# The remainder of each weight tile by an accumulating transfer on Pool instead of a VectorE subtraction

## The chip, the cores and the metric

The kernel runs on one core of one Trainium2 chip. The metric is the device time of one execution in microseconds; the time before is the median of three runs. An engine's name stands for its in-order instruction queue: TensorE (PE, with its weight loads PEld), VectorE (DVE), ScalarE (ACT), GpSimd (POOL) and SyncE (SP). SyncE only issues transfers; the transfers themselves run on 16 DMA engines.

## The reference

A decoder trunk of two layers over 512 tokens and 1024 channels, in float32. Layer one mixes tokens with a Mamba-2 state-space block (SSD, 8 groups, chunks of 128 tokens), layer two with latent attention (MLA, 8 heads). Each mixing is followed by a layer norm and by a gated feed-forward part (FFN) of hidden width 2816 with a causal depthwise convolution, and that by another layer norm:

```python
for i in range(DEPTH):
    mix = ssd_mixer(h, ...) if i < N_A_LAYERS else mla_attention(h, ..., *shared_kv, cos, sin)
    h = layer_norm(DN_ALPHA * h + mix, ln_mix_g[i], ln_mix_b[i])
    h = layer_norm(DN_ALPHA * h + conv_ffn(h, ...), ln_ffn_g[i], ln_ffn_b[i])
    if i == N_A_LAYERS - 1:
        shared_kv = mla_shared_kv(h, ...)
```

## The kernel before, in words

All matrix products run on TensorE with operands of type float32r. To keep float32's precision, each operand is held as two tiles: a cast to float32r (hi) and the remainder (lo = value - hi). A product is then three passes: hi x hi, lo x hi and hi x lo. In `mm_a` the weight is the stationary operand and the order is: all k tiles with the weight's hi, all with its lo, all with its hi against the activations' lo. In `mm_b` the activations are stationary, and the three passes come for each k tile in turn.

The weights come from HBM as a stream of 228 tiles of up to 128 x 1024 (512 KB), in the fixed order in which they are used. `WStream` handles one tile in three steps:

- `_load` (L47): SyncE issues the transfer of tile i into a staging buffer (`wst`, 3 buffers).
- `_split` (L60, L61): ScalarE casts the stage into `wh`, then VectorE writes `wl` = stage - `wh`. `wh` and `wl` have 6 buffers each (`nb`).
- `get` / `retire`: TensorE uses `wh` and `wl`; `retire` frees their buffers.

After each split, the loads of the next three tiles are issued, so a load waits until all that reads its staging buffer's former tile is done. `ahead` runs splits up to `la` = 4 tiles ahead of the tile in use, as far as the 6 buffers allow. SyncE's queue keeps the order in which the program is written; the queues of the other engines are ordered by a scheduler that plans with costs. SyncE's queue also carries other loads: x at the start, `W` (the decay rows of a group, L501), the layer norms' parameters and the output.

The stream runs through the blocks in this order: in SSD z of group 0 and dt (four small tiles, consumed while x arrives), then for each group four tiles of the convolved projections, two of z and up to two of the output projection; six tiles of the output projection at the end (`OUT_LAST`). Then the first FFN: twice 22 up tiles and 12 down tiles. Then MLA: six tiles of the joint down projection (`dw`), two for the rope part of q (`rw`), two for the values (`vw`), eight of 640 columns for the heads (`hw`), eight of the output projection. Then the second FFN.

In the last part of each FFN (`piece`) the six down tiles stay until the last 128 tokens are done; they are retired one by one there. Each block's first products are with tokens that are already normalised (`k.pend` holds the transposes of the last token tile): the FFN does its first four tiles by halves of the tokens.

The layer norm takes sums on VectorE, squares on ScalarE, and the reciprocal root on Pool (`ln_apply`, L155 and L156); SSD has such a step for each group (L587, L588). Pool has no other part in the main work.

Of the kernel before, what the change touches and what calls it, by code (L numbers as in the profile page):

```python
# [14 lines left out]
ALU = mybir.AluOpType  # L15
# [15 lines left out]
class WStream:  # L31
# [19 lines left out]
    def _split(self, nst=None):  # L51
        nc = self.k.nc
        i = self.split
        while self.loaded <= i:
            self._load()
        f = self.items[i][1]
        s = self.st.pop(i)
        h = self.k.wh.tile([P, 1024], F32R, name="wh")
        l = self.k.wl.tile([P, 1024], F32R, name="wl")
        nc.scalar.copy(h[:, :f], s[:, :f])  # L60
        nc.vector.tensor_tensor(l[:, :f], s[:, :f], h[:, :f], op=ALU.subtract)  # L61
        self.w[i] = (h, l)
        self.split += 1
        while self.loaded < min(len(self.items), self.split + (self.nst if nst is None else nst)):
            self._load()
# [17 lines left out]
class K:  # L83
# [28 lines left out]
        return self.ps.tile([P, 512], F32, name="ps")  # L112

    def mm_a(self, out, w, xts, ts, c0=None, m=P, first=True, last=True):
        """out[m, ts] = W^T x over the k tiles; w = (hi, lo) of [P, nk, m]."""
        nc = self.nc
        wh, wl = w
        nk = len(xts)
        for p, (w, x) in enumerate(((wh, 0), (wl, 0), (wh, 1))):
            for k in range(nk):  # L120
                nc.tensor.matmul(out, w[:, k, :], xts[k][:, x, ts], start=first and p == 0 and k == 0,  # L121
                                 stop=last and p == 2 and k == nk - 1, skip_group_check=True)

    def mm_b(self, out, xt, tsl, wh, wl, start, stop):
        """out[tok, n] += x W for one k tile."""
        nc = self.nc
        nc.tensor.matmul(out, xt[:, 0, tsl], wh, start=start, stop=False, skip_group_check=True)  # L127
        nc.tensor.matmul(out, xt[:, 0, tsl], wl, start=False, stop=False, skip_group_check=True)  # L128
        nc.tensor.matmul(out, xt[:, 1, tsl], wh, start=False, stop=stop, skip_group_check=True)  # L129
# [5 lines left out]
        self.gb = t  # L135

    def add_mix(self, i, hf, ps, scale, last=False):
        """h half <- scale * h half + ps; the last time with its sum over channels."""
        hs = self.h[:, i, hf * 512:(hf + 1) * 512]
        kw = {}  # L140
        if last:
            if i not in self.st:
                self.st[i] = self.lns.tile([P, 6], F32, name="lnst", bufs=4)
            kw["accum_out"] = self.st[i][:, hf:hf + 1]
        self.nc.vector.scalar_tensor_tensor(hs, hs, scale, ps, op0=ALU.mult, op1=ALU.add, **kw)  # L145
# [16 lines left out]
            nc.vector.scalar_tensor_tensor(hv[:, sl], hv[:, sl], rstd, self.gb[:, 1, sl], op0=ALU.mult, op1=ALU.add)  # L162

    def ln_last(self, i, bs, out):
        """The last tile: its second half comes in two pieces (bs); the squares are taken
        about the mean c of the first three quarters, so that only the last quarter's are
        left at the end: var = mean((h - c)^2) - (mu - c)^2."""
        nc = self.nc
        hv = self.h[:, i, :]
        s = self.st.pop(i)  # L170
# [21 lines left out]
            nc.sync.dma_start(out[:, sl], hv[:, sl])  # L192

    def transpose_h(self, i):
        """h[:, i, :] -> ht[k][:, 0/1, i*128:(i+1)*128]."""
        nc = self.nc
        ts = slice(i * P, (i + 1) * P)
        for q in range(2):
            b = self.bank()
            for j in range(4):  # L200
                k = q * 4 + j
                nc.tensor.transpose(b[:, j * P:(j + 1) * P], self.h[:, i, k * P:(k + 1) * P], self.ident)  # L202
            bv = b.rearrange("p (k t) -> p k t", k=4)
            hi = self.htt[:, q * 4:(q + 1) * 4, 0, ts]
            nc.scalar.copy(hi, bv)
            nc.vector.tensor_tensor(self.htt[:, q * 4:(q + 1) * 4, 1, ts], bv, hi, op=ALU.subtract)
# [5 lines left out]


def ffn_items(up, down):
    """up: [44, P, 1024] tiles; down: [2816, 1024]."""
    it = []
    dv = down.rearrange("(k p) n -> p k n", p=P)
    for r in range(2):
        for c in range(r * 11, r * 11 + 11):
            it.append((up[c], 1024))  # L220
            it.append((up[c + HT], 1024))
        for hf in range(2):
            for j in range(0, 11, 2):
                n = min(2, 11 - j)
                k0 = r * 11 + j
                it.append((dv[:, k0:k0 + n, hf * 512:(hf + 1) * 512], n * 512))
    return it
# [17 lines left out]


def ffn(k, ws, base, cwp, gb, la=2, out=None):
    """h <- LN(alpha h + conv_ffn(h)); expects ht of h complete up to k.pend."""
    nc, tc = k.nc, k.tc
    with ExitStack() as c:  # L250
        pool = lambda n, b: c.enter_context(tc.tile_pool(name=n, bufs=b))
# [6 lines left out]
        for r in range(2):  # L258
# [5 lines left out]

            c0 = r * 11
            if k.pend:
                # the first pairs by halves of the tokens: the last tiles are still to come
                bs = [k.bank() for _ in range(4)]
                wv = lambda i: [x.rearrange("p (k m) -> p k m", k=KT) for x in ws.get(n + i)]
                for i in range(4):  # L270
# [78 lines left out]
ZDT = ((0, 1), (1, 4), (4, 7), (7, 8))  # L349
OUT_AT = {2: (0, 1), 3: (2, 3), 4: (4, 5), 5: (6, 7), 7: (8, 9)}  # L350
WARM = 8
# bulk matmul time (us) to let pass before the chain steps s1..s5 and the cumulative dt step
LAG = [18, 13, 6, 5, 11, 13]
OUT_LAST = (10, 11, 12, 13, 14, 15)
DRAM = bass.MemoryType.DRAM


def ssd_items(xbc, zdt, zw, ow):
    """xbc: [32, P, 1024] tiles (16 x, 8 B, 8 C); zdt: [P, 8, 288] (z of group 0, dt); zw: [1024, 2048]; ow: [2048, 1024]."""
    it = []  # L360
    zv = zw.rearrange("(k p) n -> p k n", p=P)
    for a, b in ZDT:
# [13 lines left out]
def ssd(k, ws, base, xT, x, cwp, hv, ngp, gb):  # L376
    nc, tc = k.nc, k.tc
    with ExitStack() as cx:
# [5 lines left out]
        ytp = pool("yt", 7)  # L384
        drp = pool("drp", 1, space=DRAM)

        # parameters
        cw = one.tile([P, 32, 5], F32, name="cw4")
        ng = one.tile([P, 16], F32, name="ng")
        hb = one.tile([P, 3, NH], F32, name="hb")  # L390
# [5 lines left out]
        nc.gpsimd.memset(ones, 1.0)  # L396

        xv = xT.rearrange("(k p) n -> p k n", p=P)
        # the tensor engine's clock rises while the first loads are under way
        warm = k.bank()  # L400
        for _ in range(WARM):
            nc.tensor.matmul(warm[:, :P], k.ident, k.ident, start=True, stop=True)
# [83 lines left out]
            D.update(cum=cum, ecum=ecum, ecl=ecl, wend=wend, cumd=cumd)  # L486

        def bc(t, g, c0, c1, part=P):
            """per-head columns of group g for chunks c0..c1, broadcast over the head's channels."""
            return t[:, c0:c1, g * HPG:(g + 1) * HPG].unsqueeze(3).broadcast_to([P, c1 - c0, HPG, HD])  # L490

        def v4(t, c):
# [117 lines left out]
            todo.append((key, fn, t0, after))  # L610

        def tick(dt_us):
            """account for bulk matmuls; run the chain steps whose inputs had time to come."""
            T[0] += dt_us
            again = True
            while again:
# [29 lines left out]
                tick(2.6)  # L646

        def z_dt():
            """z of group 0 and dt, along with the arrival of x."""
            zs = G[0]["z"] = one.tile([P, NT, GC], F32, name="zs")  # L650
            bs = [k.bank() for _ in range(NT)]
            c = -1
# [49 lines left out]
        for g in range(NG):  # L702
# [31 lines left out]
                k.load_ln(gb)  # L734
            if g in OUT_AT:
                out_block(OUT_AT[g], g == min(OUT_AT))
        # the last rows of out_proj: those at hand before the last chain ends
        early, late = OUT_LAST[:4], OUT_LAST[4:]
        w = [ws.get(n[0] + j) for j in range(len(OUT_LAST))]
        pre = {}  # L740
# [35 lines left out]


def mla_items(dw, vw, rw, hw, ow):
    """dw [6,P,1024]; vw [256,1024]; rw [384,512]; hw [8,P,640]; ow [1024,1024]."""
    it = [(dw[j], 1024) for j in range(4)] + [(dw[j][:, :768], 768) for j in (4, 5)]  # L780
    rv = rw.rearrange("(k p) n -> p k n", p=P)
    it += [(rv[:, 0:2, :], 1024), (rv[:, 2:3, :], 512)]
# [5 lines left out]


def rope_tables(k, pos, freq):  # L790
    """cos, sin of positions x frequencies, [P, NT, 32] with tokens on partitions."""
    nc = k.nc
    c = k.const
    N = NT * 32
# [26 lines left out]


def rope(k, dst, ps, i, nh, tmp):
    """dst[P, nh, 64] = rope of ps[P, nh, 64] (token layout) for token tile i."""
    nc = k.nc
    cos = k.cs[:, 0, i, :].unsqueeze(1).broadcast_to([P, nh, 32])
    sin = k.cs[:, 1, i, :].unsqueeze(1).broadcast_to([P, nh, 32])
# [336 lines left out]
```

## Time and profile before

| | before |
|---|---|
| median of three runs, us | 1373.17 (1373.12 to 1376.29) |
| span of the profiled execution, us | 1373.7 |
| instructions | 17806 |
| VectorE busy, us | 858.3 (62%) |
| ScalarE busy, us | 627.5 (46%) |
| Pool busy, us | 45.4 (3%), 76 instructions |
| moved by transfers | 135.19 MB |
| mean granted TensorE clock | 0.999 |

One execution was profiled. Its busy times count an engine's instructions, not the issuing of transfers. A matmul's end in these rows is modelled, so TensorE's busy time also holds part of its short waits; a gap between the starts of its instructions is the safer sign. In a timeline row stand the start, the duration, the engine, the line, the operation with its output and inputs, the number of such instructions merged, and in brackets the idle time before it with what ended that. In a row of waits stand who waited, for whom, the sum in us, how often, and the longest. Line numbers are those of the kernel before.

### The profile page before, as it was taken

How to read it: one execution, taken by the hardware profiler on the slowest of the kernel's cores; microseconds unless marked ns; L12 is line 12 of the kernel's file. 1: busy time of each engine (PE TensorE's matmuls, PEld its weight loads, DVE VectorE, ACT ScalarE, POOL GpSimd, SP SyncE). 2: the span in 40 equal slices, each digit the busy share in tenths (PEclk: the TensorE clock that was granted, in tenths of full speed). 3: DMA queues.
4: the chain of work that ended last, by engine and by line, in shares of the span. 5: the costliest groups of instructions: out<-in, count | busy, mean ns of one | idle time of the engine just before them, and what ended most of it. 6: DMA issues, size and time to landing. Idle time of an engine off the chain costs nothing.

```text
span 1373.7 us, 17806 instructions
## 1 busy us (share of the span) xinstructions
PE 1359.9 (99%) x7001; PEld 1158.3 (84%) x7001; DVE 858.3 (62%) x1333; ACT 627.5 (46%) x1167; POOL 45.4 (3%) x76
## 2 busy tenths in 40 slices
PE   8999999999999999999999999999999999999997
PEld 8898898898898988888888889778898888888886
DVE  6867676677676766435655366987576552456534
ACT  5668647547554544313443134665254442244421
POOL 0000000000001000000000021000000000000002
PEclk9999999999999999999999999999999999999999
DMA  7532322323321522223232222311052323332211
GB/s 237 186 127 74 108 93 93 108 81 119 108 97 37 177 92 92 100 89 104 93 106 85 85 87 64 91 47 62 31 169 95 105 87 100 97 102 93 97 56 62
DMA packets 49652, 135.19 MB, mean 98 GB/s; under 512 B 4736, under 2 KB 12800, under 8 KB 48032
## 3 DMA queue, kind: packets, MB, share of 16 engines
q1 hardware_dynamic: 49568, 134.05, 29.5%
q8 instruction: 55, 0.90, 0.3%
q14 instruction: 29, 0.24, 0.0%
HBM read 131.87 MB, written 2.16 MB: 98 GB/s over the span
## 4 chain that ended last, share of the span: by engine, by line
PE 96%; DVE 2%; DMA 1%; POOL 0%; ACT 0%; issue 0%; SPq 0%; POOLq 0%; DVEq 0%; ACTq 0%
PE ps L121 49%; PE ps L128 12%; PE ps L127 12%; PE ps L129 12%; PE ps L982 2%; PE ps L562 2%; PE ps L1017 1%; PE ps L664 1%; PE ps L202 1%; PE ps L550 1%; PE ps L573 1%; PE ps L1004 1%; PE ps L508 1%; PE ps L529 1%; DMA W<-cumd 0%; PE ps L596 0%
## 5 line engine op out<-in xcount | busy, mean ns | idle before, releaser
L121 PE MATMUL ps<-ht,wh 128*128 128x512 f32 (+1 forms) x2048 | 464.2, 377 | 0.0
L121 PEld LDWEIGHTS ps<-ht,wh 128*128 128x128 f32 x2048 | 367.7, 188 | 69.4
L61 DVE TENSOR_TENSOR wl<-wst,wh 128x1024 fp32r<-128x1024 f32 (+2 forms) x228 | 266.5, 1174 | 166.0 <-ACT wh L60 165.4
L60 ACT CAST wh<-wst 128x1024 fp32r<-128x1024 f32 (+2 forms) x228 | 229.9, 1013 | 239.3 <-PE ps L129 185.0
L121 PE MATMUL ps<-ht,wl 128*128 128x512 f32 (+1 forms) x1024 | 239.3, 376 | 0.0
L121 PEld LDWEIGHTS ps<-ht,wl 128*128 128x128 f32 x1024 | 184.7, 188 | 35.0
L128 PE MATMUL ps<-wl,gt 128*128 128x512 f32 (+1 forms) x363 | 140.4, 387 | 0.0
L127 PE MATMUL ps<-wh,gt 128*128 128x512 f32 (+1 forms) x363 | 140.0, 386 | 0.0
L129 PE MATMUL ps<-wh,gt 128*128 128x512 f32 (+1 forms) x363 | 138.6, 382 | 0.0
L237 DVE SCALAR_TENSOR_TENSOR acc<-ps,cw,acc 128x511 f32<-128x511 f32 x88 | 65.5, 746 | 99.5 <-ACT acc L236 99.5
L145 DVE SCALAR_TENSOR_TENSOR h<-h,ps 128x512 f32<-128x512 f32 x95 | 63.1, 683 | 73.7 <-PE ps L129 73.6
L429 DVE SCALAR_TENSOR_TENSOR cv<-ps,cw,cv 128x511 f32<-128x511 f32 (+2 forms) x96 | 71.1, 744 | 38.8 <-ACT cv L427 37.9
L236 ACT ACTIVATE acc<-ps,cw 128x512 f32<-128x512 f32 x88 | 68.3, 777 | 39.8 <-PE ps L121 39.8
L127 PE MATMUL ps<-wh,ht 128*128 128x256 f32 (+2 forms) x288 | 85.6, 297 | 0.0
L129 PE MATMUL ps<-wh,ht 128*128 128x256 f32 (+2 forms) x288 | 84.1, 292 | 0.0
L128 PE MATMUL ps<-wl,ht 128*128 128x256 f32 (+2 forms) x288 | 84.1, 292 | 0.0
L127 PEld LDWEIGHTS ps<-wh,gt 128*128 128x128 f32 x363 | 68.1, 188 | 14.8
L129 PEld LDWEIGHTS ps<-wh,gt 128*128 128x128 f32 x363 | 68.2, 188 | 14.3
L128 PEld LDWEIGHTS ps<-wl,gt 128*128 128x128 f32 x363 | 68.3, 188 | 12.8
L243 ACT CAST gt<-acc 128x512 fp32r<-128x512 f32 x44 | 27.3, 621 | 98.8 <-DVE acc L242 98.8
L241 ACT ACTIVATE acc<-acc 128x512 f32<-128x512 f32 x44 | 27.8, 632 | 87.0 <-DVE acc L238 87.0
L238 DVE SCALAR_TENSOR_TENSOR acc<-ps,cw,acc 128x510 f32<-128x510 f32 x88 | 65.6, 748 | 2.8
(222 smaller groups left out, 1709.7 us busy)
## 6 DMA issues: line engine op xcount, KB each, us to landing
wst<-in_up_dram SPq DMA_DIRECT2D x88, 512.0 KB, 3.5
wst<-in_down_dram SPq DMA_DIRECT2D x40, 512.0 KB, 3.6
wst<-in_xbc_dram SPq DMA_DIRECT2D x32, 512.0 KB, 3.8
W<-cumd SPq DMA_DIRECT2D x8, 1024.0 KB, 4.7
wst<-in_sow_dram SPq DMA_DIRECT2D x16, 512.0 KB, 3.3
wst<-in_zw_dram SPq DMA_DIRECT2D x14, 512.0 KB, 3.4
lngb<-in_gb_dram SPq DMA_DIRECT2D x4, 1024.0 KB, 5.8
wst<-in_aow_dram SPq DMA_DIRECT2D x8, 512.0 KB, 3.4
```

Of the source, the lines that this page charges most:

```text
L60: nc.scalar.copy(h[:, :f], s[:, :f])
L61: nc.vector.tensor_tensor(l[:, :f], s[:, :f], h[:, :f], op=ALU.subtract)
L121: nc.tensor.matmul(out, w[:, k, :], xts[k][:, x, ts], start=first and p == 0 and k == 0, stop=last and p == 2 and k == nk - 1, skip_group_ ...
L127: nc.tensor.matmul(out, xt[:, 0, tsl], wh, start=start, stop=False, skip_group_check=True)
L128: nc.tensor.matmul(out, xt[:, 0, tsl], wl, start=False, stop=False, skip_group_check=True)
L129: nc.tensor.matmul(out, xt[:, 1, tsl], wh, start=False, stop=stop, skip_group_check=True)
L145: self.nc.vector.scalar_tensor_tensor(hs, hs, scale, ps, op0=ALU.mult, op1=ALU.add, **kw)
L236: nc.scalar.activation(a, b, AF.Identity, bias=cw[:, ch, 3:4], scale=cw[:, ch, 2:3])
L237: nc.vector.scalar_tensor_tensor(a[:, 1:], b[:, :SEQ - 1], cw[:, ch, 1:2], a[:, 1:], op0=ALU.mult, op1=ALU.add)
L238: nc.vector.scalar_tensor_tensor(a[:, 2:], b[:, :SEQ - 2], cw[:, ch, 0:1], a[:, 2:], op0=ALU.mult, op1=ALU.add)
L241: nc.scalar.activation(ag, ag, AF.Silu)
L429: nc.vector.scalar_tensor_tensor(t[:, d:], b[:, :SEQ - d], cw[:, ch, 3 - d:4 - d], t[:, d:], op0=ALU.mult, op1=ALU.add)
```

## The change

`_split` keeps the cast. The subtraction on VectorE is replaced by two steps: ScalarE writes minus the cast of the stage into `wl` (the same rounding to float32r, of -s), and a transfer issued from Pool's queue adds the stage onto `wl` in place. The staging buffer is now read by ScalarE twice and by that transfer. The rest of the diff takes comments out and is left out here.

```diff
         nc.scalar.copy(h[:, :f], s[:, :f])
-        nc.vector.tensor_tensor(l[:, :f], s[:, :f], h[:, :f], op=ALU.subtract)
+        nc.scalar.activation(l[:, :f], s[:, :f], AF.Copy, scale=-1.0)
+        nc.gpsimd.dma_start(l[:, :f], s[:, :f], accum_op=ALU.add)
         self.w[i] = (h, l)
```

## The prediction

> **What bounds the kernel now.** I read the page first: busy shares, the chain that ended last, the groups, the transfers. The columns of the transfer rows are count, KB each and median us from issue to landing.
>
> ```profile
> PE 1359.9 (99%) x7001; PEld 1158.3 (84%) x7001; DVE 858.3 (62%) x1333; ACT 627.5 (46%) x1167; POOL 45.4 (3%) x76
> ...
> PE 96%; DVE 2%; DMA 1%; POOL 0%; ACT 0%; issue 0%; SPq 0%; POOLq 0%; DVEq 0%; ACTq 0%
> ...
> L61 DVE TENSOR_TENSOR wl<-wst,wh 128x1024 fp32r<-128x1024 f32 (+2 forms) x228 | 266.5, 1174 | 166.0 <-ACT wh L60 165.4
> L60 ACT CAST wh<-wst 128x1024 fp32r<-128x1024 f32 (+2 forms) x228 | 229.9, 1013 | 239.3 <-PE ps L129 185.0
> ...
> q1 hardware_dynamic: 49568, 134.05, 29.5%
> ...
> wst<-in_up_dram SPq DMA_DIRECT2D x88, 512.0 KB, 3.5
> W<-cumd SPq DMA_DIRECT2D x8, 1024.0 KB, 4.7
> wst<-in_sow_dram SPq DMA_DIRECT2D x16, 512.0 KB, 3.3
> lngb<-in_gb_dram SPq DMA_DIRECT2D x4, 1024.0 KB, 5.8
> h<-in_x_dram SPq DMA_DIRECT2D x1, 2048.0 KB, 10.6
> wst<-in_vw_dram SPq DMA_DIRECT2D x2, 512.0 KB, 4.3
> wst<-in_dw_dram SPq DMA_DIRECT2D x2, 384.0 KB, 4.2
> ```
>
> TensorE is busy for 1359.9 of 1373.7 us and is 96% of the chain, so only 13.8 us could be won at all. VectorE, which the change relieves, is busy 62% of the span and 2% of the chain. What matters is therefore whether a remainder tile (wl) still reaches TensorE in time, and whether a staging buffer (wst) comes back in time for the next load. Next I read a steady stretch of the first FFN in the timeline, the time of all engines in a stretch of the second FFN, and what SyncE's queue waits for.
>
> ```profile
> 487.21 1.98 PE L121 MATMUL ps<-ht,wl 128*128 128x512 f32 x8
> 492.65 1.98 PE L121 MATMUL ps<-ht,wl 128*128 128x512 f32 x8
> 496.47 1.05 ACT L60 CAST wh<-wst 128x1024 fp32r<-128x1024 f32 x1 [0.69 <-PE ps L121]
> 1080.00:1320.00 240.00, 240.00 (x1057) 198.20 (x1056) 122.46 (x148) 86.85 (x108) 0.00 (x0) 1.00 0.29 96
> SPq L47 <- DVE wl L61: 1048.6, 209, 32.6
> SPq L501 <- PE ps L562: 50.6, 7, 9.2
> ```
>
> From one wl pass to the next is 492.65 - 487.21 = 5.44 us: TensorE takes a weight tile each 5.44 us. The cast at 496.47 waited for TensorE to leave the buffers of the tile six before it (nb=6), so its wl is wanted five tiles later, over 27 us on. SyncE's loads wait 1048.6 us in sum for the VectorE subtraction: with three staging buffers, the pass that reads the stage last sets when each load may start. In steady state a load has three tiles, 16.3 us, for everything.
>
> **The change, part by part.** *VectorE* loses 228 subtractions, 266.5 us. TensorE visibly waits for VectorE at one place, in SSD:
>
> ```profile
> 107.36 0.70 PE L573 MATMUL ps<-st,cv 128*128 128x256 f32 x2 [2.10 <-DVE yT L600]
> PEld ps L573 <- DVE yT L600: 2.5, 1, 2.5
> ```
>
> That is 2.10 us by the matmul's row and 2.5 by that of the weight load; I take the latter as the greatest gain.
>
> *ScalarE* gains 228 passes of -s, the same size as its casts: 229.9 us, from 627.5 to 857 (62%). *Pool* gains 228 transfer issues. *The 16 DMA engines* gain 228 transfers that read the stage, read wl and write wl.
>
> **T, the time from a finished -s pass to a landed remainder, is the unknown.** No row has an accumulating transfer or one issued by Pool. From below: a plain load of the same 512 KB takes 3.3 us. From above: the 2048 KB load of h takes 10.6 us, more bytes than the three streams of 512 KB. Nearest are the 1024 KB rows, 4.7 and 5.8 us, since an accumulation reads 1024 KB; I take the slower and round up for Pool's issue: T = 6.0 us. The Trainium skill, DMA: Bandwidth & Descriptors, section Anatomy of one DMA — SWDGE (gpsimd) path, gives 2.0 us plus bytes at 436 GB/s for a transfer issued by Pool; counting both reads that is an estimate of 4.4 us, by which the bursts below would cost 20.8 us instead of 35.8.
>
> *Steady state* costs nothing: load 3.5 + cast and -s 2.1 + T fit into 16.3 us up to T = 10.7, and wl has 27 us. The cost lies where tiles are needed in a burst. There a load first waits for the accumulation of the tile three before it, then its own accumulation follows: T counts twice.
>
> *Start.* The third tile (864 columns) is cast, and TensorE reaches its wl:
>
> ```profile
> 10.08 0.92 ACT L60 CAST wh<-wst 128x864 fp32r<-128x864 f32 x1
> 11.43 0.69 PE L664 MATMUL ps<-wl,ht 128*128 128x288 f32 x4
> ```
>
> With the second tile's -s (0.92) ahead of it, its own cast, its -s (0.92 each) and T, wl lands at 12.84 + T: a stall of T + 1.4 = 7.4 us. SyncE's queue also holds the last load of x behind the fourth weight load, which waits for the first accumulation; those columns of x come into use last, behind this stall.
>
> *MLA, down projection.* All six wl buffers are held until the FFN's last tokens, then six tiles are wanted in quick succession, with three staged. The first two casts, the fifth (768 columns, as the sixth), and TensorE at the sixth's wl:
>
> ```profile
> 803.61 2.19 ACT L60 CAST wh<-wst 128x1024 fp32r<-128x1024 f32 x2
> 813.66 0.82 ACT L60 CAST wh<-wst 128x768 fp32r<-128x768 f32 x1
> 817.29 0.34 PE L128 MATMUL ps<-wl,ht 128*128 128x384 f32 x1
> ```
>
> Three casts and three -s of 1.05 from 803.61 end at 809.91; then T, the load of the sixth tile 4.2, its two passes 1.64, and T: 815.75 + 2T against 817.29. Stall 2T - 1.5 = 10.5 us.
>
> *MLA, values.* The second value tile's load waits for the staging buffer of the first rope tile. The rope tile's cast, that load, and TensorE at the wl of the load's tile:
>
> ```profile
> 837.34 1.05 ACT L60 CAST wh<-wst 128x1024 fp32r<-128x1024 f32 x1 [0.83 <-PE ps L129]
> 840.55 0.38 SPq L47 DMA_DIRECT2D wst<-in_vw_dram  x1
> 849.84 0.39 PE L128 MATMUL ps<-wl,cT 128*128 128x512 f32 x1
> ```
>
> 837.34 + 2.1, T, load 4.3, two passes 2.1, T: 845.84 + 2T. Stall 2T - 4.0 = 8.0 us.
>
> *First tiles of each FFN.* Three tiles are staged, the fourth waits for the first one's buffer.
>
> ```profile
> 440.11 2.96 ACT L60 CAST wh<-wst 128x1024 fp32r<-128x1024 f32 x3 [3.11 <-PE ps L129]
> 455.61 1.12 PE L121 MATMUL ps<-ht,wl 128*128 128x256 f32 x8
> 999.01 2.95 ACT L60 CAST wh<-wst 128x1024 fp32r<-128x1024 f32 x3 [3.11 <-PE ps L129]
> 1013.63 1.12 PE L121 MATMUL ps<-ht,wl 128*128 128x256 f32 x8
> ```
>
> 440.11 + 2.1 + T + 3.5 + 2.1 + T = 447.81 + 2T against 455.61: 2T - 7.8 = 4.2 us. Likewise 1006.71 + 2T against 1013.63: 2T - 6.9 = 5.1 us.
>
> *Last down-projection tile of each FFN.* Here the tile has been loaded long before, and T counts once.
>
> ```profile
> 777.56 0.62 ACT L60 CAST wh<-wst 128x512 fp32r<-128x512 f32 x1 [1.74 <-PE ps L129]
> 792.43 1.03 PE L202 MATMUL ps<-ident,h 128*128 128x128 f32 x8
> ```
>
> The second piece of 33 matmuls ends at 792.43; at 5.44/24 = 0.227 us a matmul the first begins at 777.47 and reaches its last wl at 784.5. That lands at 777.56 + 1.24 + T: T - 5.7 = 0.3 us, twice 0.6.
>
> *SSD.* All engines over 250 us of it, and the same matmuls of two groups in the chain:
>
> ```profile
> 150.00:400.00 250.00, 250.00 (x1473) 221.60 (x1473) 178.90 (x244) 151.52 (x362) 6.44 (x10) 1.00 0.30 99
> ```
>
> ```profile
> 208.67 1.30 PE ps L573 x6
> ...
> 262.34 1.30 PE ps L573 x6
> ```
>
> ScalarE is busy 151.5 of 250 us, and a group, 262.34 - 208.67 = 53.7 us, has up to eight tiles, so 8.4 us more of ScalarE work: it stays below 80%. If one -s stands ahead of each group's chain it costs 1.05 x 8 = 8.4 us; if the shorter VectorE work ends the stall shown above it gains 2.5 us. Every tile's buffers come from far ahead, so I take + 1. The W load stands in SyncE's queue behind weight loads that now wait longer; it waits 50.6/7 = 7.2 us for TensorE today, more than the delay of T + 1.05 - 1.2 = 5.9 us, so it is covered; without that cover each of the eight groups could lose what T exceeds 7.3 us by.
>
> *Pool's queue.* The cast, and with it the -s, can wait long for TensorE:
>
> ```profile
> ACT wh L60 <- PE ps L129: 185.0, 55, 8.5
> ```
>
> A transfer waits in Pool's queue for its -s, so up to 8.5 us; behind it stand the small layer norm steps (L155, L587). They need ScalarE's squares, which stand in ScalarE's queue behind that same cast, so I take 0.
>
> The sum: 7.4 + 10.5 + 8.0 + 4.2 + 5.1 + 0.6 = 35.8 us for the bursts (11T - 30.2), with SSD 36.8. Against the profiled execution: span 1373.7 + 36.8 = 1410.5; the median of the runs, 1373.17, is 0.5 us below that span, so 1410 us. Ends: at T = 3.3 the bursts cost 4.7 + 5.1 + 2.6 = 12.4, less 2.5: 1383 us. At T = 10.6 they cost 86.4, plus 8.4: 1468 us.
>
> **The rivals.**
>
> *The DMA engines become the bound.* Per tile they are busy 0.29 x 5.44 = 1.58 us in the FFN, which leaves 3.86. An accumulation that costs as much as two loads (3.2) fits, barely; one that costs three (4.7: two reads and a write, one after the other) makes 6.3 us per tile. Then the FFNs' 88 + 40 full and 8 half tiles lose 0.86 us a full one, 114 us, and the bursts, with T midway between 6.0 and 10.7 at some 8.4, about 62: about 1550 us; more if it is slower still. For it: no cover is left once the engines are full, and no row prices the adding. Against it: the queue is at 29.5%. The Trainium skill, Collectives: The Full Stack, section The bandwidth ceiling: the fold count and why AG ≠ RS ≠ AR, lays the halved rate of an adding transfer to its second source read and not to the addition. By that rule the price is two loads, the 3.2 us above, and this rival fails; no run here shows it.
>
> *Not slower.*
>
> ```profile
> out_dram<-h SPq DMA_DIRECT2D x7, 256.0 KB, 2.0
> ```
>
> A short T: all bursts together, less the 2.5 us won, fall below 4.1 us (0.3%, about what a measurement of this kernel can tell from no change) once T is under about 2.1 us, since little but start (T + 1.4) and down projection (2T - 1.5) then remains. At T = 2 that is 3.4 us: 1377 us. For it: 256 KB stores of h land in 2.0 us. Against it: the accumulation reads four times those bytes, and no 512 KB row above lands under 3.3.
>
> *Pool's queue holds the layer norms.* If Pool's order puts a waiting transfer ahead of the layer norm steps at the ends of the four blocks, each could lose up to 8.5 us: 34 on top of 36.8, 1445 us. The common order of ScalarE's queue speaks against it.
>
> **How the numbers follow.** The forecast with T between 3.3 and 10.6 has 0.62; the DMA bound 0.21; not slower 0.13; Pool's queue 0.04. The predicted time is that of the likeliest, 1410, whose own range is 1383 to 1468. To leave out no more than 2 in 10, the range goes down to 1376, into the unslowed case, and up to 1560, past the DMA bound at three loads; beyond it lie the slower half of that rival and the lower part of the other. Faster by over 0.3% has 0.03 (it would need nearly all that VectorE can give back and a hidden T), within 0.3% 0.10, slower 0.87.
>
> **What would show it.** Right: the transfer rows list wl from wst with 5 to 7 us to landing (T less the pickup); SyncE's loads wait for that transfer instead of VectorE; ScalarE near 857 us, VectorE near 592; TensorE with new idle spots at the start, near 815, 850, 455 and 1014, waiting for wl, and none within the FFNs. Wrong: if TensorE idles all through the FFNs, or the DMA share reaches 0.9 there, the DMA bound holds; if landing is under 2.5 us, the change is hidden; if layer norm steps on Pool start late while ScalarE's squares are done, it is Pool's queue.

## The result, and the profile after

The changed kernel takes 1445.18 us in the median (1443.22 to 1449.27) against 1374.73 us (1373.12 to 1377.75) for the kernel before in the same comparison: +70.5 us, a ratio of 1.0515 (95% interval 1.0492 to 1.0538). The direction was forecast, the size was not: +36.8 us. Line numbers of the changed kernel are one higher than before from L62 on (L61 is now the -s pass, L62 the Pool transfer).

The page of the changed kernel:

```profile
span 1444.4 us, 18285 instructions
...
PE 1386.6 (96%) x7001; PEld 1174.7 (81%) x7001; DVE 621.1 (43%) x1105; ACT 827.8 (57%) x1395; POOL 240.3 (17%) x304
...
q0 software_dynamic: 32832, 114.44, 44.5%
...
wl<-wst POOLq DMA_DIRECT2D x205, 512.0 KB, 5.6
wst<-in_up_dram SPq DMA_DIRECT2D x88, 512.0 KB, 4.9
W<-cumd SPq DMA_DIRECT2D x8, 1024.0 KB, 6.1
```

The engines changed the way that was worked out, though not by the same amounts: VectorE is busy for 621 us (592 reckoned) and ScalarE for 828 us (857 reckoned), since busy time counts overlapping instructions once, so rows do not simply add up; VectorE's other 1105 instructions take 0.59 us in the mean, before and after. The new transfers land 5.6 us after their issue. In this trace an issue follows 0.3 us after the end of its -s pass (median), so T, the time from a finished -s pass to a landed remainder, is 5.9 to 6.0 us in the median, as assumed. Two things were not in the sum. The loads got slower (an up tile 3.5 to 4.9 us, W 4.7 to 6.1). And TensorE, whose instructions are as many as before, has 26.7 us more of busy time; its idle time grew from 13.8 to 57.8 us, by 44.0; the two make the 70.7 us between the spans.

The waits of TensorE and of SyncE's queue (sum, times, longest), and then the whole machine in three stretches of the changed kernel (stretch, length, busy times, granted clock, DMA share, GB/s):

```profile
PE ps L129 <- DMA wl<-wst: 13.6, 7, 4.7
PE ps L122 <- DMA wl<-wst: 9.1, 7, 2.7
PE ps L665 <- DMA wl<-wst: 5.8, 1, 5.8
PE ps L574 <- DVE yT L601: 4.4, 1, 4.4
PE ps L509 <- DVE cv L433: 3.9, 1, 3.9
SPq L47 <- DMA wl<-wst: 1252.0, 224, 32.8
```

```profile
0.00:100.00 100.00, 81.83 (x389) 70.69 (x390) 41.29 (x76) 59.93 (x99) 16.73 (x28) 0.91 0.87 223
145.00:440.00 295.00, 295.00 (x1750) 261.85 (x1749) 165.58 (x247) 211.02 (x459) 43.73 (x54) 1.00 0.71 173
520.00:800.00 280.00, 280.00 (x1234) 231.31 (x1233) 94.52 (x131) 155.91 (x188) 45.60 (x53) 1.00 0.87 197
```

From 145 to 440 us and from 520 to 800 us TensorE never idles, though the DMA engines are busy for 0.71 and 0.87 of the time. In the first 100 us it idles for 18. TensorE issues the same matmuls in both kernels, in the same order but for some 40 of 7001, so the start of a matmul after, less its start before, is the loss up to there:

| part | shift at its end, us | lost in the part, us | forecast, us |
|---|---|---|---|
| first tiles (matmul at 22.25 before, 29.94 after) | 7.7 | 7.7 | 7.4 |
| rest of SSD's groups 0 and 1 (109.52, 144.42) | 34.9 | 27.2 | 1, for all of SSD |
| SSD's groups 2 to 7 (440) | 34.9 | 0.0 | |
| first tiles of FFN1 (457.65, 498.61) | 41.0 | 6.1 | 4.2 |
| rest of FFN1 (792.43, 833.61) | 41.2 | 0.2 | 0.3 |
| MLA, down projection (828.06, 881.05) | 53.0 | 11.8 | 10.5 |
| MLA, values (876.98, 939.37) | 62.4 | 9.4 | 8.0 |
| rest of MLA (1004.00, 1068.66) | 64.7 | 2.3 | 0 |
| first tiles of FFN2 (1016.03, 1086.67) | 70.6 | 5.9 | 5.1 |
| rest of FFN2 (1299.91, 1370.55) | 70.6 | 0.0 | 0.3 |

Next the places where SSD loses it. First the changed kernel's timeline: ScalarE, VectorE, TensorE and SyncE, then three rows of the kernel before.

```profile
58.78 1.06 ACT L61 ACTIVATE wl<-wst 128x1024 fp32r<-128x1024 f32 x1 [3.36 <-DMA wst<-in_zw_dram]
59.75 0.61 ACT L432 ACTIVATE th<-cv 128x512 f32<-128x512 f32 x1
60.39 0.69 DVE L433 SCALAR_TENSOR_TENSOR cv<-th,cv 128x512 f32<-128x512 f32 x1 [5.69 <-ACT th L432]
61.23 1.18 PE L509 MATMUL ps<-cv 128*128 128x128 f32 x8 [3.94 <-DVE cv L433]
...
50.12 1.06 PE L469 MATMUL ps<-tri,dta 128*32 128x128 f32 x8
65.62 1.04 ACT L60 CAST wh<-wst 128x1024 fp32r<-128x1024 f32 x1
66.55 0.57 ACT L473 COPY cv<-ps 32x512 f32<-32x512 f32 x1
67.15 0.34 SPq L475 DMA_DIRECT2D cumd<-cv  x1
73.30 0.34 SPq L502 DMA_DIRECT2D W<-cumd  x1
79.68 1.28 ACT L522 ACTIVATE W<-W,cum 128x128 f32<-128x128 f32 x4 [7.76 <-DMA W<-cumd]
86.82 1.22 PE L551 MATMUL ps<-wx,bk 128*128 128x256 f32 x2 [2.17 <-DVE wx L542]
89.83 7.09 PE L563 MATMUL ps<-xdt,W 128*128 128x64 f32 x32 [1.79 <-DVE W L535]
```

```profile
46.35 0.56 ACT L472 COPY cv<-ps 32x512 f32<-32x512 f32 x1
53.46 2.16 ACT L521 ACTIVATE W<-W,cum 128x128 f32<-128x128 f32 x7 [1.36 <-DMA W<-cumd]
69.08 3.68 PE L562 MATMUL ps<-xdt,W 128*128 128x64 f32 x32
```

The first four rows are one chain. A -s pass waits 3.36 us at the head of ScalarE's queue for a late load; the tanh of a convolution stands behind it, though its input is there; VectorE waits for the tanh, TensorE for VectorE (3.94 us). The next rows are the decay chain. TensorE has the sums at 51.5 us, but the copy of cT stands behind the cast of another late tile and runs at 66.55 us (46.35 before); the 64 KB transfer of cumd takes 6.1 us until W's load may be issued, and W, there at 79.68 us, was there at 53.46 us before. TensorE then waits 1.9, 2.2 and 1.8 us, and its 32 decay matmuls take 7.09 us where they took 3.68 with no other work in them. That is the clock:

```profile
62.20:65.60 3.40, 3.40 (x12) 2.81 (x11) 1.84 (x3) 2.13 (x3) 0.26 (x1) 0.50 0.99 201
86.10:99.80 13.70, 11.19 (x49) 10.47 (x50) 11.04 (x17) 12.05 (x21) 2.55 (x3) 0.50 0.50 96
```

The granted clock is exactly half in these two stretches and in six more, each a multiple of 3.4 us long but the last, which the end cuts off. There are 46.2 us of half clock in all, 5.7 before. The Trainium skill, TensorE: Matmul & The Clock Gate, section Part 1: The HAM clock gate, describes a gate that passes half the pulses after an idle window of 3413 ns. The trace agrees with the half and with the length of the window. It does not show a fully idle window ahead of these two stretches: in the 3.4 us ahead of each, TensorE was still busy for 0.94 and 1.10 us.

```profile
58.76:62.17 3.41, 0.94 (x8) 0.97 (x9) 1.74 (x3) 3.18 (x4) 0.84 (x1) 1.00 1.08 281
82.65:86.07 3.42, 1.10 (x4) 0.68 (x4) 1.74 (x4) 3.42 (x11) 0.00 (x0) 1.00 0.85 345
```

The 13.7 us begin within the second of the three waits, which lasts from 84.65 to 86.82 us; the third lies inside them. The same page, the Trainium skill's TensorE: Matmul & The Clock Gate, prices half clock in its section Terms at the time times one minus the share of pulses passed. By that price the 40.5 us more would be, as an estimate, at most 20.3 us of the 26.7 us of added busy time; an experiment below shows that such time need not be won back.

### The profile page after: what moved, and what is told of

It reads as the page before. It is cut to its first block, busy times and chain, and to the rows that moved or that the text cites. A ratio compares the mean times of both kernels' runs of the same rounds, so it can differ in the third digit from the quotient of the medians.

```text
span 1444.4 us, 18285 instructions
## 1 busy us (share of the span) xinstructions
PE 1386.6 (96%) x7001; PEld 1174.7 (81%) x7001; DVE 621.1 (43%) x1105; ACT 827.8 (57%) x1395; POOL 240.3 (17%) x304
## 3 DMA queue, kind: packets, MB, share of 16 engines
q0 software_dynamic: 32832, 114.44, 44.5%
q1 hardware_dynamic: 49568, 134.05, 28.3%
## 4 chain that ended last, share of the span: by engine, by line
PE 83%; DMA 10%; issue 4%; ACT 3%; DVE 0%; POOL 0%; POOLq 0%; SPq 0%; DVEq 0%; ACTq 0%
PE ps L122 43%; PE ps L129 11%; PE ps L128 11%; PE ps L130 10%; DMA wl<-wst 5%; PE ps L983 2%; PE ps L563 2%; DMA wst<-in_xbc_dram 1%; DMA W<-cumd 1%; PE ps L1018 1%; ACT wh L60 1%; DMA wst<-in_up_dram 1%; ACT wl L61 1%; PE ps L551 1%; PE ps L574 1%
## 5 line engine op out<-in xcount | busy, mean ns | idle before, releaser
L122 PE MATMUL ps<-ht,wh 128*128 128x512 f32 (+1 forms) x2048 | 469.5, 380 | 4.6 <-ACT ytmp L582 3.7
L122 PEld LDWEIGHTS ps<-ht,wh 128*128 128x128 f32 x2048 | 371.9, 191 | 75.6 <-ACT ytmp L582 3.9
L62 POOL DMA_DIRECT2D wl<-wst x228 | 196.7, 863 | 1056.2 <-ACT wl L61 986.2
L61 ACT ACTIVATE wl<-wst 128x1024 fp32r<-128x1024 f32 (+2 forms) x228 | 232.4, 1020 | 186.1 <-PE ps L129 145.5
L128 PE MATMUL ps<-wh,ht 128*128 128x256 f32 (+2 forms) x288 | 87.0, 303 | 0.4 <-DVE ctok L892 0.4
L130 PE MATMUL ps<-wh,ht 128*128 128x256 f32 (+2 forms) x288 | 85.7, 298 | 0.0
L237 ACT ACTIVATE acc<-ps,cw 128x512 f32<-128x512 f32 x88 | 68.0, 774 | 15.7 <-PE ps L122 13.7
L242 ACT ACTIVATE acc<-acc 128x512 f32<-128x512 f32 x44 | 27.8, 632 | 66.5 <-DVE acc L239 66.5
```

The lines of the kernel that those rows point to most:

```text
L61: nc.scalar.activation(l[:, :f], s[:, :f], AF.Copy, scale=-1.0)
L62: nc.gpsimd.dma_start(l[:, :f], s[:, :f], accum_op=ALU.add)
L237: nc.scalar.activation(a, b, AF.Identity, bias=cw[:, ch, 3:4], scale=cw[:, ch, 2:3])
```

## The experiments

Each number is a median with the ratio to the kernel before, measured beside it, and its 95% interval; that kernel's median lay between 1373.2 and 1374.7 us. "After plus" is an edit of the changed kernel, "before plus" of the kernel before.

**Two theories of ScalarE and of the staging buffers.** *b_act*, before plus the -s pass, whose result VectorE overwrites:

```diff
+        nc.scalar.activation(l[:, :f], s[:, :f], AF.Copy, scale=-1.0)
         nc.vector.tensor_tensor(l[:, :f], s[:, :f], h[:, :f], op=ALU.subtract)
```

> The kernel before with the 228 passes of -s added on ScalarE; VectorE then overwrites wl with the true remainder, and no accumulating transfer is issued. ScalarE theory: 20 us or more of the loss appear in SSD, 1395 us or more. Staging and traffic theories: nearly nothing, 1373 to 1380 us, since ScalarE stays under 80% busy everywhere.

1376.54 us, 1.0022 (1.0011 to 1.0034): all of ScalarE's added work costs 3 us. *a_ssd4*, after plus a fourth staging buffer in SSD (to make room for it, two pairs of small tiles share a buffer, in *b_traffic* below too):

```diff
-        t = self.k.wst.tile([P, 1024], F32, name="wst")
+        pool = self.k.wst2 if i < 66 and i % 4 == 3 else self.k.wst
+        t = pool.tile([P, 1024], F32, name="wst")
...
-        while self.loaded < min(len(self.items), self.split + (self.nst if nst is None else nst)):
+        while self.loaded < min(len(self.items), self.split + (4 if self.loaded < 66 else 3)):
```

> The changed kernel with a fourth staging buffer for the 66 weight tiles of SSD (the other blocks keep three). Staging theory: between 22 and 144 us of the span the stage is held until its accumulation has landed, so the next load is late, and the cast that waits for it at the head of ScalarE's queue holds back the convolution and decay steps behind it; a fourth buffer takes 5.4 us out of that loop for each tile, so of the 27 us lost in SSD's first two groups at most 10 stay, and the time falls from 1445 to 1415-1430 us. ScalarE theory (the 66 passes of -s themselves delay SSD's steps) and traffic theory (the accumulations slow the loads of W and x): the loss stays, 1440 us or more.

1442.51 us, 1.0483 (1.0446 to 1.0521). A miss: some 3 us won instead of 15 to 30, and the interval overlaps that of the changed kernel, so even these are not certain. Its shift at the end of SSD is 28.3 us instead of 34.9. The transfers of its first 100 us suggest why:

```profile
wl<-wst POOLq DMA_DIRECT2D x14, 512.0 KB, 7.2
wst<-in_xbc_dram SPq DMA_DIRECT2D x12, 512.0 KB, 6.3
```

More was under way at once, and each took longer: 7.2 us for an accumulation (5.7 in the changed kernel's first 100 us), 6.3 for a load (5.9). Its DMA engines were busy for 0.95 of the first 60 us (0.91 in the changed kernel), so a fourth buffer found little room there.

**Traffic, and traffic with the stage held.** *b_hold*, before plus an accumulating transfer of `wh` onto the stage after VectorE has made `wl`: the load on the DMA engines and the wait for the stage are those of the change, the remainder is early. *b_traffic*, before plus a transfer in SSD alone, of `wh` onto one tile that nobody reads:

```diff
         nc.vector.tensor_tensor(l[:, :f], s[:, :f], h[:, :f], op=ALU.subtract)
+        nc.gpsimd.dma_start(s[:, :f], h[:, :f], accum_op=ALU.add)                    # b_hold
+        if i < 66:                                                                   # b_traffic
+            nc.gpsimd.dma_start(self.k.jk[:, :f], h[:, :f], accum_op=ALU.add)
```

> The kernel before, with VectorE's remainder, and behind it an accumulating transfer from Pool that adds wh onto the stage just read: the same traffic, and the stage is held until it lands, but wl is ready as early as before and ScalarE has no second pass. Staging theory: most of the SSD loss and half of the bursts (T counts once instead of twice): 1395 to 1425 us. ScalarE theory: 1373 to 1385 us. Traffic theory: as in the run with the traffic alone.

> The kernel before, and for each of SSD's 66 tiles an accumulating transfer from Pool that adds wh onto a tile that nothing reads: the traffic of the change in SSD, with no stage held, wl as early as before and no second pass on ScalarE. Traffic theory: 20 us or more are lost in SSD, 1395 us or more. Staging and ScalarE theories: 1373 to 1382 us.

b_hold: 1434.85 us, 1.0438 (1.0421 to 1.0456), above the 1395 to 1425 expected; its shift is 31 us at the end of SSD. So a late remainder is not needed for SSD's loss; a late stage and the traffic do it. Behind SSD, where T counted once was expected to halve the loss, it still loses 30 us (36 in the changed kernel): 3.3 and 3.0 us at the first tiles of the FFNs instead of 6.1 and 5.9, but 23.7 us in MLA, as much as the 23.5 of the changed kernel. b_traffic: 1407.77 us, 1.0236 (1.0218 to 1.0255), but 18 us of it come from my choice of a single target, which lets only one transfer be under way. TensorE's longest wait, and Pool and VectorE of that kernel:

```profile
PE ps L600 <- DVE st L561: 18.3, 1, 18.3
```

```profile
127.04 0.20 POOL L591 TENSOR_SCALAR ss<-ss 128x4 f32<-128x4 f32 x1
130.80 0.75 DVE L433 SCALAR_TENSOR_TENSOR cv<-ps,cw,cv 128x511 f32<-128x511 f32 x1 [24.89 <-ACT cv L431]
```

The small step on `ss` (L591) stands in Pool's queue behind a row of transfers that go one at a time, and VectorE idles for 24.89 us. Ahead of that the shift was 11.2 us, and TensorE's wait there alone adds the 18.3 us of the first row. Without it traffic costs 11 us by that shift and 16 by the medians, not 27; neither theory's number was met.

**Where in the stream.** Three kernels use the transfer for some tiles and VectorE's subtraction for the others:

```diff
+        if i < 20:                                              # p_start
+        if i >= 20:                                             # p_late
+        if 20 <= i < 66 or 72 <= i < 134 or 166 <= i < 228:     # p_far
             nc.scalar.activation(l[:, :f], s[:, :f], AF.Copy, scale=-1.0)
             nc.gpsimd.dma_start(l[:, :f], s[:, :f], accum_op=ALU.add)
+        else:
+            nc.vector.tensor_tensor(l[:, :f], s[:, :f], h[:, :f], op=ALU.subtract)
```

> The accumulating transfer makes the remainder of tiles 0 to 19 alone; VectorE's subtraction makes the other 208. Start theory: all of SSD's loss comes from the first two groups, where the stream of weights has no lead yet and the DMA engines are nearly full. In the trace of after, TensorE's shift against before stands at 34.8 us by 109 us of before's time and stays there until 445 us; so this kernel should give 1373 + 35 = 1408 us (1400 to 1414), with some 24 us of half clock before 145 us and the shift constant from there to the end. Rival, loss spread over all accumulations: 20 of 228 tiles give about 6 us plus the 7.7 of the first tiles, 1382 to 1388.

> The complement: VectorE's subtraction for tiles 0 to 19, the accumulating transfer for tiles 20 to 227. Start theory: the 34.8 us of SSD are gone, what is left is FFN1's first tiles 6, MLA's down and value tiles and the steps between them 24, FFN2's first tiles 6: 1373 + 36 = 1409 us (1402 to 1416). The two kernels' losses then add to the 70.5 us of the full change. Rival, SSD is slowed by the accumulations wherever they are in it: 1425 us or more.

> The accumulating transfer only where the stream has a lead: SSD tiles 20 to 65, FFN1 tiles 72 to 133, FFN2 tiles 166 to 227 (170 of 228 tiles); VectorE makes the remainder of the first 20 tiles, of FFN1's first six, and of the whole MLA and FFN2's first six. Theory that the loss is latency at the places where the stream starts without a lead: 1373 to 1380 us, though the DMA engines still carry the accumulations, with their busy share over 0.8 in both FFNs. Rival, the DMA engines' load itself costs time: the loss goes with the number of accumulations, 170/228 of 70 us, 1415 to 1430 us.

p_start 1406.05 us, 1.0231 (1.0215 to 1.0247); p_late 1413.34 us, 1.0281 (1.0267 to 1.0295); p_far 1375.95 us, 1.0007 (0.9997 to 1.0018). The losses of p_start and p_late, 31.4 and 38.7 us, add to 70.1 of the 70.5. And 170 of the 228 transfers cost nothing that can be measured:

```profile
145.00:440.00 295.00, 295.00 (x1691) 258.59 (x1691) 163.02 (x251) 200.97 (x439) 46.96 (x58) 1.00 0.66 165
520.00:800.00 280.00, 280.00 (x1236) 231.11 (x1235) 87.14 (x128) 139.89 (x169) 45.54 (x53) 1.00 0.80 182
```

TensorE is full in both stretches with the DMA engines at 0.66 and 0.80, so there neither their load nor the count of transfers costs anything.

**Delay or traffic at the start.** The same 20 tiles with a delay but without the traffic, three ways: by three like subtractions on Pool (*p_pool*); by a transfer of 8 columns while VectorE makes the others (*p_tiny*); by two such transfers, one behind the other (*p_tiny2*).

```diff
         if i < 20:
-            nc.scalar.activation(l[:, :f], s[:, :f], AF.Copy, scale=-1.0)
-            nc.gpsimd.dma_start(l[:, :f], s[:, :f], accum_op=ALU.add)
+            for _ in range(3):                                                             # p_pool
+                nc.gpsimd.tensor_tensor(l[:, :f], s[:, :f], h[:, :f], op=ALU.subtract)
+            nc.scalar.activation(l[:, :8], s[:, :8], AF.Copy, scale=-1.0)                  # p_tiny, p_tiny2
+            nc.vector.tensor_tensor(l[:, 8:f], s[:, 8:f], h[:, 8:f], op=ALU.subtract)
+            nc.gpsimd.dma_start(l[:, :8], self.k.zero, accum_op=ALU.add)                   # p_tiny2 alone
+            nc.gpsimd.dma_start(l[:, :8], s[:, :8], accum_op=ALU.add)
```

> As the kernel with the transfer on tiles 0 to 19 alone (1406.05 us), but with the remainder of these tiles made by three like subtractions on Pool's own arithmetic in place of the transfer: about the same delay between the cast and the remainder, the staging buffer held as long, and no traffic on the DMA engines. By three passes of 1 to 2 us each the delay is 3 to 6 us. Theory, delay and traffic together: without the traffic the loads stay near 3.5 us, three staging buffers give a tile every 3.5 us against a use of one in 5.4, so the stream builds its lead and only the first tiles' delay is paid: 1380 to 1388 us. Rival, delay and the held buffer alone: 1398 to 1406 us.

> As the kernel with the transfer on tiles 0 to 19 alone (1406.05 us), but the transfer makes only 8 of a tile's columns (4 KB in place of 512 KB) and VectorE subtracts the rest: nearly no traffic, a delay of one transfer of any size (2.5 to 4.5 us from issue to landing) and the staging buffer held as long. Traffic and delay together make the loss: the start pays 4 to 6 us, the loads stay near 3.5 us and the stream builds its lead, 1379 to 1388 us. Rival, the delay alone makes it: 1396 to 1406 us. Pool's three passes could not tell, since at 2.31 us a pass they took 6.9 us a tile, more than a tile's use of 5.4 us.

> As the last, with two such small transfers one behind the other on the same columns (the first adds zeros): the delay is 5 to 9 us, at least that of the full transfer (5.6 us), still nearly without traffic; Pool's queue waits for the first before it issues the second, 4 to 5 us a tile. Traffic and delay together: the start pays 7 to 10 us, little more is lost, 1382 to 1392 us. Rival, the delay alone: 1404 us or more.

p_pool took 1442.25 us, 1.0501 (1.0484 to 1.0519), and tells nothing of traffic, since a pass over a full tile took 2.48 us and three of them 7.4, more than the 5.44 us in which TensorE uses a tile. p_tiny took 1379.23 us, 1.0038 (1.0025 to 1.0050), and p_tiny2 1392.17 us, 1.0129 (1.0113 to 1.0145). Pool's passes in p_pool, and the transfers of p_tiny, p_tiny2 and p_start in their first 100 us:

```profile
L63 POOL TENSOR_TENSOR wl<-wst,wh 128x1024 fp32r<-128x1024 f32 x48 | 118.0, 2477 | 16.5 <-ACT wh L60 14.8
```

```profile
wst<-in_xbc_dram SPq DMA_DIRECT2D x13, 512.0 KB, 4.3
wl<-wst POOLq DMA_DIRECT2D x20, 4.0 KB, 3.3
cumd<-cv SPq DMA_DIRECT2D x1, 64.0 KB, 1.6
```

```profile
wst<-in_xbc_dram SPq DMA_DIRECT2D x12, 512.0 KB, 3.7
wl<-zero POOLq DMA_DIRECT2D x18, 4.0 KB, 2.7
wl<-wst POOLq DMA_DIRECT2D x18, 4.0 KB, 2.8
cumd<-cv SPq DMA_DIRECT2D x1, 64.0 KB, 3.6
```

```profile
wst<-in_xbc_dram SPq DMA_DIRECT2D x12, 512.0 KB, 5.7
wl<-wst POOLq DMA_DIRECT2D x14, 512.0 KB, 5.8
cumd<-cv SPq DMA_DIRECT2D x1, 64.0 KB, 5.1
```

In the median the last issue came 0.3 us (p_tiny), 4.1 us (p_tiny2) and 0.3 us (p_start) after the -s pass, and its transfer had landed 3.7, 7.3 and 6.1 us after that pass; these are the delays. Though its delay is even the longer, p_tiny2 loses 18.1 us and p_start 31.4: of p_start's loss at most some 18 us go with the delay and the held stage, and the other 13 need the traffic. The split is no finer than that, since in p_tiny2 Pool's queue also waits between its two transfers. Neither of my two theories had the split: p_tiny2 lies at the upper edge of the first one's range and far below the second's.

What the delay does is best seen in the time that three staging buffers need for a tile, (load + cast + -s + delay)/3, against the 5.44 us in which TensorE uses one. Before it is (4.5 + 1.05 + 1.2)/3 = 2.3, with VectorE's subtraction as the last reader; p_tiny (4.3 + 1.25 + 3.7)/3 = 3.1; p_tiny2 (3.7 + 1.25 + 7.3)/3 = 4.1; p_start (5.7 + 2.1 + 6.1)/3 = 4.6; p_pool, by its passes alone, 7.4. The losses are 0, 5.2, 18.1, 31.4 and 68.5 us. They grow long before that time reaches 5.44 us. My reading is that the stream then takes too long to build its lead; no run shows the lead by itself. The traffic adds through the loads (4.5 us before, 5.7 in p_start) and perhaps through the small transfer of cumd (1.6 and 5.1, but 3.6 in p_tiny2 nearly without traffic).

**Through which queue.** *a_ct*, after plus the copy of cT on VectorE; *a_lag*, after plus the decay step earlier in program order:

```diff
-            nc.scalar.copy(cT[:NH, :], b2[:NH, :])           # a_ct
+            nc.vector.tensor_copy(cT[:NH, :], b2[:NH, :])
-LAG = [18, 13, 6, 5, 11, 13]                                 # a_lag
+LAG = [18, 13, 6, 5, 11, 2]
```

> The changed kernel, with one small copy (32x512 of the decay sums, cT) moved from ScalarE to VectorE; nothing else. Queue theory: in ScalarE's order this copy stands behind the casts of tiles 13 and 14, which wait for their loads, so it ran at 66.55 us although TensorE had its input at about 51.5 us; with it go the two small transfers and W. On VectorE it runs near 52 us, W is there before ScalarE has done the copy of bk at 71.4 us, and the passes over W start at about 72 in place of 79.7 us. TensorE then reaches the state and decay products at 81.7 us with little to wait for: the waits of 1.9, 2.2 and 1.8 us and the half-clock stretch of 13.7 us behind them go, 5.9 + 6.9 = 12.8 us, of which some may come back at the next cast: 1434 us (1430 to 1439). Rival, the loads alone set the pace of the first groups and the copy's place is no matter: 1443 to 1447 us.

> The changed kernel, with the decay sums' step (its matmuls, the cT copy, the two small transfers, W) set two weight tiles earlier in program order (its lag 2 in place of 13); nothing else. On VectorE the copy stood behind the conv steps just as it stood behind the casts on ScalarE, so the engine was not the matter but the place in the order. Queue theory: the copy now stands behind two casts fewer, runs near 54 us in place of 66.55, W is there by 68 in place of 79.7 us, and group 0's waits for it (1.9, 2.2, 1.8 us) and the half-clock stretch of 13.7 us behind them go: 1434 us (1430 to 1440). Rival, the arrival of the weights sets the pace of the first groups whatever else waits: TensorE waits for weights instead, 1443 to 1447 us.

a_ct: 1445.92 us, 1.0521 (1.0503 to 1.0540), no gain. Its copy on VectorE, and then a_lag's copy and the first of its passes over W:

```profile
66.02 0.67 DVE L473 COPY cv<-ps 32x512 f32<-32x512 f32 x1
```

```profile
50.14 0.56 ACT L473 COPY cv<-ps 32x512 f32<-32x512 f32 x1
67.34 1.28 ACT L522 ACTIVATE W<-W,cum 128x128 f32<-128x128 f32 x4 [2.79 <-DMA W<-cumd]
```

On VectorE the copy ran at 66.02 us: there it stands behind convolution steps that wait for ScalarE, so another engine changed nothing. Put earlier in the order it ran at 50.14 us and W's passes began at 67.34 instead of 79.68 us; a_lag took 1437.06 us, 1.0452 (1.0436 to 1.0469), and its shift at the end of SSD was 24.8 us instead of 34.9. So the decay chain's place behind late tiles is worth 8 us by the medians, 10 by the shift, of SSD's 27. The 11 us expected of each of the two were not reached, though a_lag lies within its range of 1430 to 1440 us; what remains is left to late weights and late convolutions, which no run tells apart.

**The clock.** *a_fill*, after plus idle matmuls in group 0's waits, into columns that the next matmul overwrites (14 ahead of the B.C products, 7 and 7 ahead of the state products, 6 ahead of the decay products). An earlier kernel of this kind, *a_warm*, had them into a bank that VectorE still read, and twice as long as I had reckoned: it made new waits of 5.3 and 5.9 us.

```diff
+                    for _ in range(7 if g == 0 and c != 1 else 0):
+                        nc.tensor.matmul(o[:, :P], k.ident, k.ident, start=True, stop=True)
                     nc.tensor.matmul(o, S["bk"][:, c * P:(c + 1) * P], S["wx"][:, c, :], start=True, stop=True)
```

> The changed kernel, with idle matmuls (128x128, identity by identity into columns of a PSUM bank that nobody reads) put into group 0's waits: 28 ahead of the B.C products, 14 ahead of the state products, 14 ahead of the third of them, 14 ahead of the decay products; by rows of 0.13 us each they fill most of the waits of 3.9, 1.9, 2.2 and 1.8 us. Clock theory: TensorE's clock halves because of these gaps; the half-clock stretches at 62 us (3.4 us) and 86 us (13.7 us) go, and the time falls by half of them, 7 to 9 us: 1437 us (1433 to 1440). Rival, the gaps cost only themselves and the low clock follows from something else: half-clock time as before, 1445 us or a little more.

> The changed kernel, with idle matmuls in group 0's waits again, now about half as many and each into columns that the next real matmul overwrites, so that none adds a wait for a reader: 14 ahead of the B.C products, 7 ahead of the state products, 7 ahead of the third, 6 ahead of the decay products. By the last run one takes 0.23 us at full clock, so they fill 3.2 of 3.9, 1.6 of 1.9, 1.6 of 2.2 and 1.4 of 1.8 us. Clock theory: the half-clock stretches at 62 us (3.4 us) and 86 us (13.7 us) go, half of 17.1 us is won: 1437 us (1433 to 1441). Rival, the low clock is not due to the gaps: the stretches stay, 1445 us or more.

a_warm 1456.27 us, 1.0608 (1.0584 to 1.0632); a_fill 1448.19 us, 1.0541 (1.0521 to 1.0562). The stretches of half clock at 62 and 86 us are gone in a_fill, but one of 6.8 us came at 91 us, within the wait of the first row:

```profile
93.35 1.22 PE L555 MATMUL ps<-wx,bk 128*128 128x256 f32 x2 [6.46 <-DVE wx L544]
96.93 4.24 PE L569 MATMUL ps<-xdt,W 128*128 128x64 f32 x32
```

The decay matmuls take 4.24 instead of 7.09 us, and the shift at the end of SSD is 33.0 instead of 34.9 us; the later parts are not faster, and the whole is not. The filling also moved the order on VectorE (the product with W now stands ahead of wx), so the one wait grew from 2.2 to 6.5 us. That gaps bring the low clock fits this; that the low clock has a price of its own in the end time, as I expected with 8.5 us, is not shown.

## Why the prediction was wrong in size

*Right.* T: 6.0 assumed, 5.9 to 6.0 measured in the median. That it fits so well is partly luck: it was the slower of two rows of other transfers, rounded up, and among the first 20 tiles it lies anywhere from 4.8 to 8.8 us. The lower estimate of 4.4 us that the prediction set beside it was too short. The start 7.4, measured 7.7. Steady state 0, measured 0 in SSD's groups 2 to 7 and in both FFNs, and p_far confirms it. The last down tiles 0.6, measured 0.2. VectorE's 266 us brought nothing that shows: the wait for yT in SSD that they might have ended sooner is 4.4 us after and 2.1 before. The DMA engines are not the bound: the transfers' 44.5% of 1444.4 us for 114.44 MB are 2.94 us of all sixteen engines for 512 KB, near the 3.2 of two loads and far from the 4.7 of three. The Trainium skill, Collectives: The Full Stack, section The bandwidth ceiling: the fold count and why AG ≠ RS ≠ AR, lays the halved rate of a ReduceScatter to the second source read that its add needs, and not to the adding. The 2.94 us agree with that.

*The step that failed* is "SSD": "Every tile's buffers come from far ahead, so I take + 1", and with it "so it is covered" for the W load. It was read from the stretch 150 to 400 us and from two groups at 208 and 262 us, and there it holds: the shift stays at 34.9 us. It was then applied to all eight groups. The row that should have been read is that of the first 100 us of the kernel before:

```profile
0.00:100.00 100.00, 96.14 (x566) 85.74 (x567) 74.06 (x118) 62.97 (x133) 2.57 (x12) 1.00 0.53 181
```

The DMA share is 0.53 there (0.87 after), not 0.30, the stream has only its first tiles in hand, and a tile that needed about 2.3 us of three staging buffers now needs (5.9 + 2.1 + 6.0)/3 = 4.7. The term was mis-sized by 26 us: 27.2 instead of 1. Runs p_start and p_late put it into the first 20 tiles, p_tiny2 splits it into delay and traffic, and a_lag shows one of its ways, the in-order queue. W did come late, at 79.68 us instead of 53.46, but through the copy in ScalarE's queue and through cumd, not behind weight loads in SyncE's queue, where the prediction had looked for cover.

*Sized too small.* The terms of the down projection, the values and the first tiles of the FFNs were 27.8 us in sum, and 33.2 us are measured. The stalls came where they were forecast, and TensorE waits for wl there. With the median loads of the trace after (4.9, 5.1, 5.2: each 0.9 to 1.4 more) the same formulas give 11.4 for the down projection, 8.9 for the values, 5.6 and 6.5 for the first tiles of the FFNs, 32.4 in sum, against 11.8, 9.4, 6.1 and 5.9 measured. Single paths do not bear out that the loads are the reason. For the sixth tile of the down projection the load took 3.4 us, less than assumed, and the two times T were 8.4 and 7.0 us. For the second value tile the load took 6.4 us and T 4.9 us twice; TensorE was 6.5 us late there, and the rest of the 9.4 came behind it, where the clock is at half from 908.7 to 915.5 us. And b_hold lost as much in MLA with the remainder made early. So how these terms divide between load, T and clock stays open. The rest of MLA had no term: 1.5 of its 2.3 us are one more wait for a late remainder, at 1036 us.

*The rivals.* Not slower and the DMA bound did not come. The third, Pool's queue, named 1445 us, the time that was measured, but that is chance. The layer norm steps on Pool still wait for ScalarE's squares:

```profile
POOL lnst L156 <- ACT lnjunk L155: 88.2, 15, 10.6
```

Its mechanism did appear once, in b_traffic, where the transfers went one at a time.

No version here beats the kernel before; p_far equals it.

## What to carry to other kernels

A longer hand-over cost nothing here where the stream had its lead, and 6 to 12 us at each place where it started anew, 27 more in SSD's first groups; so cost it at every start, from rows of that start, and never from a steady stretch. For a ring of buffers compare (load + all readers)/buffers with the time of use: a lead builds only from the difference. Transfers that are off the critical path can still slow the loads beside them, here by 1.4 us for 512 KB, and in an in-order queue one late tile delays work that has nothing to do with it.

## What was not expected of the hardware

The granted clock fell to 0.50, in units of 3.4 us, though TensorE was still busy for 0.94 and 1.10 us of the 3.4 us ahead, between waits of 1.9 to 3.9 us. Beside the accumulating transfers a 64 KB transfer took 6.1 us to land (1.6 before), four times as long, while 512 KB loads took 1.4 us more; in p_tiny2, nearly without traffic, it took 3.6 us, so the traffic is not shown to be the only cause. A subtraction of 128 x 1024 on Pool took 2.48 us, where VectorE's took 1.22. An accumulating transfer of 4 KB landed after 2.7 to 3.3 us and one of 512 KB after 5.6, so about half of the delay did not depend on its size.
